# Other fills for the attention phase, another closing of its page pools and a staging ring of two slots, in a one-core hybrid trunk layer

## Chip, cores and metric

The kernel runs on one core of one Trainium2 chip. The metric is device time of an execution in microseconds (us), the median of several runs. A trace of one profiled execution shows what each engine did: PE is TensorE (matmuls), DVE is VectorE, ACT is ScalarE, POOL is GpSimd, SP is SyncE, which here issues most of the DMA transfers. Each engine works through its own list of instructions in order.

## What is computed

One layer over 2,064 tokens (16 meta tokens and 2,048 others) of 1,024 channels. One input projection feeds two branches; their results are joined, projected and added to the input.

```python
u = rmsnorm(h, norm_g) @ w_in
pool_in, pool_gate, c_q, c_kv, k_r, attn_gate = jnp.split(u, SPLIT_POINTS, axis=-1)
pool_out = silu(pool_gate) * pool_mixer(pool_in, pool_w, pool_scale)
# pool_mixer: 4 channel groups, mean over the last 2/4/8/16 tokens minus the token,
# then a 128x128 map per group
q  = rmsnorm(c_q,  q_norm_g)  @ w_q_b      # 4 heads, 128 plain + 64 rotary
kv = rmsnorm(c_kv, kv_norm_g) @ w_kv_b
attn = mla_attention(q_nope, q_rope, k_nope, k_rope, v, chunk_id)   # mask by chunks of 64
attn_out = silu(attn_gate) * attn
h = h + concatenate([pool_out, attn_out]) @ w_out
return rmsnorm(h, final_norm_g)[:, 16:]
```

## The kernel before

The kernel has three phases that overlap. First the columns of the input projection that attention needs (queries, keys and values compressed) are made for all tokens. Then attention goes over chunks of 64 tokens, late ones first, by groups of four chunks: the groups 5, 6, 7, 4, 3 and 2 in the order of the loop `for c in seq` (the first two groups have been done earlier). Last come the remaining 1,536 columns of the input projection ("the projection"), the pooling branch, the gates and the output projection, in blocks of 256 tokens.

One attention step is `scores(c, p)` for chunk c and head pair p: score matmuls on PE (names `s14_...`), maxima on DVE, exponentials on ACT into a page `p`, a split of it into two 16-bit halves (a page `hl`; ACT, POOL and DVE), and a transposing DMA, issued by SP, from `hl` to a page `pt`. `pv(c)` multiplies the pages by the values (`o14`), and once a group has four chunks `vproj` makes its attention result (`av`). `pv` is written a number of steps behind the scores of its chunk, the lag (0 or 1). The pages come in turn from rings that several pools make up: `set_pages` takes a list of pools with counts for (p, hl, pt), for example ATT1 = (2, 4, 2). Query preparation of a group (`qprep`, matmuls `qa`, `qp`, `qt`) is written ahead of the chunk named in QAT.

The projection works on twelve blocks of 128 columns, taken as six pairs: pairs 0 to 3 are a pooling group's channels with their gate, pairs 4 and 5 are two attention gates each. Text commands set their order, in the table PREP behind chosen chunks of attention and in the list TAIL behind attention:

- `a0` (`load_w`): the two weight blocks of pair 0 are loaded by SP into the staging ring (names `wr...`) and ACT takes their maxima; `b0` (`scale_w`): PE transposes the maxima (`wmx`), DVE works out a power of two, and ACT, DVE and POOL write the weights as two 16-bit halves (`w...`);
- `x0` (`load_x`): the 256 (272 for block 0) input columns of block 0 are loaded in two halves into the same staging ring (`yr0_0`, `yr0_4`), DVE multiplies them by the norm, ACT and POOL write two 16-bit halves (`xx`);
- `03`: block 0, pair 3 (`pair`): 24 matmuls of 128x256 for each of the two column blocks (`mp0_3` and `mp0_7`), then for a pooling group window sums on DVE (`pool_in`), a gate (`gate`), and one pair later the pooling map (`pool_out`, `pm0_3`); for attention gates, a product with the attention result;
- `o0` (`load_wo`): a slice of the output weights through the staging ring (`wor0`); ACT casts it, DVE subtracts, which gives two halves (`wo0`);
- `p0` and `q0` (`op_prep`, `op`): 128 tokens of the output projection, 48 matmuls of 128x512 (`op0_0`, `op0_1`); the residual rows go through the staging ring as well (`xr0`).

FILL says behind which chunk a pair of the list `fill` is written. A scheduler orders each engine's instructions by its own simulated times, so what is written behind a chunk may be interleaved with it. `raw` hands out staging slots: all loads go through it in turn, and one that comes round waits until the slot's last reader is done. The ring has two slots in pool c1 and, once pool mixp is open behind attention, a third.

Of the kernel before, what the change touches and what calls it, by code (L numbers as in the profile page):

```python
# [16 lines left out]
P = 128  # L17
# [21 lines left out]
B1_LAG = 1  # L39
B2_LAG = 0  # L40
ATT1 = (2, 4, 2)
ATT2 = (4, 4, 7)
ATT3 = (1, 1, 1)
NS = 6
QB = "m"
FILL = {13: 1, 12: 1, 11: 1, 9: 1}
XSC = 9
# [15 lines left out]
QAT = {22: 6, 26: 7, 30: 4, 19: 3, 15: 2}  # L63
CLOSE = 17
TAIL = """b3 a4 a5 03 b4 13 b5 04 o0 14 o1 05 o2 x2 15 o3 x3 20 o4 21 o5 o6 22 o7 g 23 p0 24 25 q0 x4
          p1 30 q1 p2 31 q2 32 p3 33 q3 34 35 p4 x5 40 q4 41 p5 42 q5 43 p6 44 q6 45 p7 x6 50 q7 51 p8 52 q8 53 p9 54 q9 55
          p10 x7 60 q10 61 p11 62 q11 63 64 65 70 71 72 p12 73 q12 p13 74 75 q13 p14 q14 p15 q15"""
PREP = {17: 'a0', 16: 'b0 x0', 15: 'a1', 14: 'b1 a2', 13: 'b2', 12: 'x1', 10: 'a3'}

# [20 lines left out]
def hymba(tc, hT, hcat, tab, w_tok, w_m, w_out, wqT, wqr, wkT, wv, pool_w,  # L90
# [453 lines left out]
    def raw(cols, name):  # L544
        n = cnt[0]
        cnt[0] += 1
        pool, b = (cpools[0], 2) if len(cpools) == 1 or n % 3 < 2 else (cpools[1], 1)
        return pool.tile([P, cols], F32, name=name, tag="wr", bufs=b, padded_shape=[P, 1088])

    def load_x(i):  # L550
        o, n = SUBS[i]
        if "x" not in cw:
            cw["x"] = kx.tile([P, 2, 4352], F16, name="xx", tag="khi", bufs=1, padded_shape=[P, 2, 4352])
        x = cw["x"][:, i % 2, :2 * KT * n].rearrange("p (a k t) -> p a k t", a=2, k=KT)
        xh, xl = x[:, 0], x[:, 1]
# [13 lines left out]
    def load_w(pi):  # L569
        for e in range(2):  # L570
            m = MORDER[2 * pi + e]
            if pi == 4:
                wr = f(cpools[1].tile([P, D], F32R, name=f"wr{m}", tag="mh", bufs=2))
            else:
                wr = raw(D, f"wr{m}")
            nc.sync.dma_start(out=wr, in_=w_m[m])
            for n in range(2):
                junk = cw["pool"].tile([P, 512], F16, name=f"wa{m}_{n}", tag="wa", bufs=1)
                nc.scalar.activation(out=junk, in_=wr[:, n * 512:n * 512 + 512], func=AF.Abs, accum_out=wmx[:, pi, e, n:n + 1])
            wts[m] = (wr, 2 * pi + e)  # L580

    def scale_w(pi):
# [7 lines left out]
        for e in range(2):  # L590
            m = MORDER[2 * pi + e]
            wr, at = wts[m]
            wp = cpools[0 if pi < 3 else 1].tile([P, 2, D], F16, name=f"w{m}")
            sc = wsc[:, at:at + 1]
# [21 lines left out]
    def pool_in(g, i, ps):  # L616
        n = SUBS[i][1]
        c1, carry = cw["pool"], cw["carry"]
        u = c1.tile([P, 16 + n], F32, name=f"u{i}_{g}", tag="u", bufs=2, padded_shape=[P, 288])
# [20 lines left out]
    def gate(m, i, ps):  # L640
        gt = cw["pool"].tile([P, G], F32, name=f"gt{i}_{m}", tag="gt", bufs=3)
        th = cw["pool"].tile([P, G], F32, name=f"th{i}_{m}", tag="th", bufs=2)
        nc.scalar.activation(out=th, in_=ps[:, :G], func=AF.Tanh, scale=whalf[:, wts[m][2]:wts[m][2] + 1])  # L643
# [15 lines left out]
    def pre_c(pool):  # L659
        cpools.append(pool)  # L660
        cw["pool"] = pool
        cw["carry"] = pool.tile([P, H, 16], F32, name="carry")
        nc.gpsimd.memset(cw["carry"], 0.0)

    def load_pw():
        pool = cw["pool"]
        pw_r = raw(H * P, "pw_r")
# [18 lines left out]
    def pair(i, pi):  # L686
        m0, m1 = MORDER[2 * pi], MORDER[2 * pi + 1]
        if i not in mixg:
            mixg[i] = cpools[i % 3 // 2].tile([P, H, G], F32, name=f"mix{i}", tag="mix", bufs=1 if i % 3 == 2 else 2)
        q0 = mproj(m0, i)  # L690
# [112 lines left out]
    c1 = None  # L803
    fill = [(0, 0), (0, 1), (0, 2), (1, 0), (1, 1), (1, 2)]
    for c in seq:
        if c in QAT:
            qprep(QAT[c])
        for p in range(2):
            step(c, p, B1_LAG if not c1 else B2_LAG)
        if c == CLOSE:  # L810
            flush()
            close_pool(att2_cm)
            set_pages((att1, ATT1), (att3, ATT3))
            c1_cm, c1 = open_pool("c1", side="right")
# [88 lines left out]
```

## Time and profile before

| | us |
|---|---|
| median of 3 runs (918.52 to 921.26) | 919.92 |
| profiled execution | 919.55 |
| its span in the profile | 917.8 |
| PE busy, whole span | 863.5 (94%) |
| DVE, ACT, POOL busy | 525.1, 454.2, 329.5 |

Three stretches of the span: up to 481 us attention goes on, from 481 to 570.5 us the projection runs without attention up to the first output matmul, and from there to 913 us projection and output projection alternate. The span lies 1.75 us below the profiled execution's own time. An idle time of an engine counts where it is on the way to the end; PE is that engine here, so its waits and the clock that it was granted are read first.

### The profile page before, as it was taken

Reading aid. Unit: us, or ns where it says so; the run is one execution under the profiler, and the core shown is the slowest. Engines: PE = TensorE matmul, PEld = TensorE weight load, DVE = VectorE, ACT = ScalarE, POOL = GpSimd, SP = SyncE. Lnnn points to the kernel's source line nnn. Section 1 sums busy time; section 2 is a strip of 40 time slices with the busy share of each in tenths; the row PEclk is TensorE's granted clock in tenths of the full one; section 3 lists DMA queues with packets and bytes.
Section 4 is the critical chain, followed back from the end, with each engine's and each line's share of the span. In section 5 each row is a group of like instructions: output and inputs, shape, how many; then the busy total and the mean of one; then the engine's idle time right before and its main releaser. Section 6 shows DMA issues by size and latency. Waiting matters only on the chain. (4 is left out here: it accounts for less than half of the span.)

```text
span 917.8 us, 16168 instructions
## 1 busy us (share of the span) xinstructions
PE 863.5 (94%) x5849; PEld 750.6 (82%) x5849; DVE 525.1 (57%) x1224; ACT 454.2 (49%) x1189; POOL 329.5 (36%) x520
## 2 busy tenths in 40 slices
PE   9899899899999999778898979999999999999996
PEld 8798778888888888666696868888888888888885
DVE  5566678857666665866854985255444443534332
ACT  6576657757767755857545763122322313223121
POOL 2576542625446442442421573221311413212020
PEclk9999999999999999979997989999999999999999
DMA  8765435967898687495572352211211211210011
GB/s 265 231 196 161 116 56 110 162 133 135 147 154 146 127 153 155 74 209 128 134 157 75 99 176 67 92 46 54 92 46 46 98 63 54 96 55 13 11 55 50
DMA packets 206955, 101.79 MB, mean 111 GB/s; under 512 B 169257, under 2 KB 196363, under 8 KB 206875
## 3 DMA queue, kind: packets, MB, share of 16 engines
q1 hardware_dynamic: 187392, 93.30, 42.8%
q10 hardware_dynamic: 19483, 7.47, 3.4%
q8 instruction: 46, 0.75, 0.4%
q14 instruction: 34, 0.28, 0.1%
HBM read 55.60 MB, written 8.43 MB: 70 GB/s over the span
## 5 line engine op out<-in xcount | busy, mean ns | idle before, releaser
L612 PE MATMUL mp<-xx,w 128*128 128x256 f16 (+1 forms) x2304 | 268.4, 276 | 11.5 <-ACT xx L565 6.3
L612 PEld LDWEIGHTS <-w 128*128 128x128 f16 x2304 | 224.6, 99 | 47.2 <-issue 12.6
L737 PE MATMUL op<-wo,mh 128*128 128x512 f32 (+1 forms) x528 | 159.3, 384 | 0.0
L464 POOL TENSOR_TENSOR hl<-p,hl 128x512 f16<-128x512 f32 (+4 forms) x104 | 102.6, 1008 | 116.4 <-ACT hl L462 115.0
L459 ACT ACTIVATE p<-s,st 128x512 f32<-128x512 f32 (+8 forms) x168 | 99.1, 599 | 68.4 <-DVE st L444 53.8
L737 PEld LDWEIGHTS op<-wo,mh 128*128 128x128 f32 x528 | 97.2, 188 | 18.6
L438 DVE TENSOR_REDUCE st<-s 128x1 f32<-128x512 f32 (+6 forms) x154 | 89.1, 590 | 17.7 <-PE s L436 16.7
L495 PE MATMUL o<-pt,vh 128*128 128x256 f16 x544 | 91.9, 273 | 2.2 <-DVE ol L498 1.2
L739 DVE TENSOR_TENSOR xr<-op,xr 128x512 f32<-128x512 f32 (+1 forms) x33 | 22.3, 676 | 117.8 <-PE op L737 117.8
L462 ACT CAST hl<-p 128x512 f16<-128x512 f32 (+6 forms) x168 | 82.2, 538 | 7.9 <-DMA pt<-hl 5.9
L495 PE MATMUL o<-pt,vl 128*128 128x256 f16 x272 | 74.1, 273 | 0.0
L741 ACT ACTIVATE osq<-xr 128x512 f16<-128x512 f32 (+1 forms) x33 | 20.3, 616 | 98.3 <-DVE xr L739 83.3
L495 PEld LDWEIGHTS <-vh 128*128 128x128 f16 x544 | 51.9, 98 | 12.1 <-issue 4.6
L643 ACT ACTIVATE th<-mp,whalf 128x256 f32<-128x256 f32 x64 | 30.1, 471 | 55.4 <-PE mp L612 52.6
L737 PE MATMUL op<-wo,ml 128*128 128x512 f32 x144 | 56.1, 390 | 0.0
L464 DVE TENSOR_TENSOR hl<-p,hl 128x512 f16<-128x512 f32 (+7 forms) x64 | 45.4, 710 | 12.7 <-ACT hl L462 12.2
L432 PE MATMUL s<-klo,qh 128*128 128x512 f32 (+9 forms) x116 | 45.0, 388 | 3.4 <-DVE gt L645 3.3
L566 POOL TENSOR_TENSOR xx<-yr,xx 128x512 f16<-128x512 f32 (+1 forms) x32 | 41.4, 1308 | 15.6 <-ACT xx L565 15.6
L562 DVE SCALAR_TENSOR_TENSOR yr<-yr,gxs,rbc 128x256 f32<-128x256 f32 (+1 forms) x64 | 34.9, 604 | 19.4 <-DMA yr<-hT_in 19.4
L737 PE MATMUL op<-wo,ml_odd 128*128 128x512 f32 (+1 forms) x120 | 45.0, 375 | 0.0
L434 PE MATMUL s<-klo,ql 128*128 128x512 f32 (+9 forms) x116 | 43.1, 371 | 0.0
L433 PE MATMUL s<-klo,qh 128*128 128x512 f32 (+9 forms) x116 | 42.7, 368 | 0.0
(213 smaller groups left out, 1807.4 us busy)
## 6 DMA issues: line engine op xcount, KB each, us to landing
xt<-hcat_in SPq DMA_DIRECT2D x16, 512.0 KB, 5.0
xr<-hcat_in SPq DMA_DIRECT2D x16, 512.0 KB, 3.7
raw<-hT_in SPq DMA_DIRECT2D x15, 512.0 KB, 4.8
out_dram<-xr SPq DMA_DIRECT2D x15, 512.0 KB, 2.6
yr<-hT_in SPq DMA_DIRECT2D x14, 512.0 KB, 3.8
wr<-w_m_in SPq DMA_DIRECT2D x12, 512.0 KB, 3.8
rb<-rd ACTq DMA_DIRECT2D x32, 128.0 KB, 4.4
wor<-w_out_in SPq DMA_DIRECT2D x8, 512.0 KB, 4.2
```

Source lines behind the costliest of these rows:

```text
L432: nc.tensor.matmul(ps[:, :w], lhsT=q(qh), rhs=kt[:, 0, 0, sl], start=True, stop=False)
L433: nc.tensor.matmul(ps[:, :w], lhsT=q(qh), rhs=kt[:, 1, 0, sl], start=False, stop=False)
L434: nc.tensor.matmul(ps[:, :w], lhsT=q(ql), rhs=kt[:, 0, 0, sl], start=False, stop=False)
L438: nc.vector.reduce_max(out=mx[:, bi:bi + 1], in_=ps[:, :w], axis=AX.X)
L459: nc.scalar.activation(out=pr[:, o:o + w], in_=pss[bi][:, :w], func=AF.Exp, bias=nb_, accum_out=sm[:, bi:bi + 1] if nb > 1 else tot)
L462: nc.scalar.copy(out=hl[:, 0, sl], in_=pr[:, sl])
L464: eng.tensor_tensor(out=hl[:, 1, sl], in0=pr[:, sl], in1=hl[:, 0, sl], op=ALU.subtract)
L495: nc.tensor.matmul(ps[:, :2 * P], lhsT=v, rhs=x, start=i == 0, stop=i == len(ops) - 1)
L562: nc.vector.scalar_tensor_tensor(out=xr[:, k - k0], in0=xr[:, k - k0], scalar=gxs[:, k:k + 1], in1=rbc, op0=ALU.mult, op1=ALU.mult)
L566: nc.gpsimd.tensor_tensor(out=xl[:, k:k + 2], in0=xr[:, k - k0:k - k0 + 2], in1=xh[:, k:k + 2], op=ALU.subtract)
L612: nc.tensor.matmul(ps[:, :n - sk], lhsT=a[:, k], rhs=x[:, k, sk:n], start=e == 0, stop=e == 3 * KT - 1)
L737: nc.tensor.matmul(ps[:, :w], lhsT=x[:, k], rhs=y[:, sl], start=i == 0, stop=i == 3 * KT - 1)
```

## The change

- The attention phase: lag 1 throughout; ATT2 and ATT3 are cut differently (their sum with ATT1 is 7, 9 and 10 pages, as before); behind chunk 28 pages come from ATT1 and ATT3 alone (4, 7, 7). Pool c1 opens behind chunk 19 (before: 17), with no flush ahead of it.
- The fills are pairs 4 and 5 of block 0 and pair 4 of block 1 (three pairs, before six); weights of pairs 4 and 5 are prepared in attention, those of pairs 0 to 3 behind it.
- The first input columns have a tile of their own in c1 (`x0`), reused later by the output projection's `mh`; later columns go to `xx` as before.
- The staging ring has two slots throughout. The last weights' second way through the `mh` slots is gone.
- The pooling branch's tiles (carry, windows, pooling weights, mix) move from c1 to mixp, which is there only behind attention.

```diff
-B2_LAG = 0
+B2_LAG = 1
-ATT2 = (4, 4, 7)
-ATT3 = (1, 1, 1)
+ATT2 = (3, 2, 3)
+ATT3 = (2, 3, 5)
-FILL = {13: 1, 12: 1, 11: 1, 9: 1}
+FILL = {15: 1, 13: 1, 11: 1}
-CLOSE = 17
-TAIL = """b3 a4 a5 03 b4 13 b5 04 o0 14 o1 05 o2 x2 15 o3 x3 20 o4 21 o5 o6 22 o7 g 23 p0 24 25 q0 x4
...
-PREP = {17: 'a0', 16: 'b0 x0', 15: 'a1', 14: 'b1 a2', 13: 'b2', 12: 'x1', 10: 'a3'}
+LASTLONG = 28
+CLOSE = 19
+TAIL = """b0 w a1 15 24 b1 25 a2 00 10 b2 20 a3 01 11 b3 21 o0 02 o1 12 o2 22 o3 03 o4 13 o5 x3 23 o6 p0 o7 g
...
+PREP = {18: 'a4', 17: 'b4 x0', 16: 'a5', 15: 'b5', 14: 'x1', 12: 'x2', 10: 'a0'}
...
-        pool, b = (cpools[0], 2) if len(cpools) == 1 or n % 3 < 2 else (cpools[1], 1)
-        return pool.tile([P, cols], F32, name=name, tag="wr", bufs=b, padded_shape=[P, 1088])
+        return cpools[0].tile([P, cols], F32, name=name, tag="wr", bufs=2, padded_shape=[P, 1088])
...
-        if "x" not in cw:
-            cw["x"] = kx.tile([P, 2, 4352], F16, name="xx", tag="khi", bufs=1, padded_shape=[P, 2, 4352])
-        x = cw["x"][:, i % 2, :2 * KT * n].rearrange("p (a k t) -> p a k t", a=2, k=KT)
+        if i == 0:
+            x = cw["pool"].tile([P, 2 * KT * n], F16, name="x0", tag="x0", bufs=1)
+        else:
+            if i == 1:
+                cw["x"] = kx.tile([P, 2, 4352], F16, name="xx", tag="khi", bufs=1)
+            x = cw["x"][:, i % 2, :2 * KT * n]
+        x = x.rearrange("p (a k t) -> p a k t", a=2, k=KT)
...
-            if pi == 4:
-                wr = f(cpools[1].tile([P, D], F32R, name=f"wr{m}", tag="mh", bufs=2))
-            else:
-                wr = raw(D, f"wr{m}")
+            wr = raw(D, f"wr{m}")
...
-            wp = cpools[0 if pi < 3 else 1].tile([P, 2, D], F16, name=f"w{m}")
+            wp = cpools[0 if pi >= 4 else 1].tile([P, 2, D], F16, name=f"w{m}")
...
-        c1, carry = cw["pool"], cw["carry"]
+        c1, carry = cpools[1], cw["carry"]
...
-    fill = [(0, 0), (0, 1), (0, 2), (1, 0), (1, 1), (1, 2)]
+    fill = [(0, 4), (0, 5), (1, 4)]
...
-            step(c, p, B1_LAG if not c1 else B2_LAG)
+            step(c, p, B1_LAG)
+        if c == LASTLONG:
+            set_pages((att1, ATT1), (att3, ATT3))
         if c == CLOSE:
-            flush()
             close_pool(att2_cm)
-            set_pages((att1, ATT1), (att3, ATT3))
             c1_cm, c1 = open_pool("c1", side="right")
             pre_c(c1)
```

How the order moves at three places (line numbers of the changed kernel are 1 to 3 higher). PE where the first input columns are first used: `mp0_0` and `mp0_8` are projection matmuls of block 0, `o15` the value product of chunk 15, `s12` and `s14` scores, `qp2` the query preparation of group 2. Before:

```order
L495 MATMUL o15_5138<-pt15_2_5087,vc_122 128x256
L612 LDWEIGHTS w0_4924
L612 MATMUL mp0_0_5423<-xx_4942,w0_4924 128x272
...
L612 LDWEIGHTS w4_4930
L612 MATMUL mp0_4_5460<-xx_4942,w4_4930 128x256
...
L432 MATMUL s12_0_0_5490<-klo_115,qh3_4218 128x384
```

Now:

```order
L347 MATMUL qp2_4954<-wrh_126,cl2_4916 128x256
L613 LDWEIGHTS w8_4738
L613 MATMUL mp0_8_5162<-x0_4750,w8_4738 128x256
...
L613 LDWEIGHTS w9_4744
L613 MATMUL mp0_9_5192<-x0_4750,w9_4744 128x256
...
L433 MATMUL s14_0_0_5225<-klo_115,qh3_4218 128x512
```

The first use stands ahead of the scores of chunk 14 where it stood ahead of those of chunk 12, and right behind the query preparation; it is of pair 4 instead of pair 0.

SP, the loads of the staging ring behind attention (weights `wr`, output weights `wor`, input columns `yr`, residual rows `xr`). Before:

```order
L576 DMA wr8_6419<-w_m_in 128x1024
L576 DMA wr9_6425<-w_m_in 128x1024
L576 DMA wr11_6437<-w_m_in 128x1024
L576 DMA wr10_6431<-w_m_in 128x1024
L679 DMA wor0_6711<-w_out_in 128x1024
L679 DMA wor1_6778<-w_out_in 128x1024
L560 DMA yr2_0_6851<-hT_in 128x4x256
L560 DMA yr2_4_6861<-hT_in 128x4x256
L679 DMA wor2_6845<-w_out_in 128x1024
L679 DMA wor3_6934<-w_out_in 128x1024
L560 DMA yr3_0_6940<-hT_in 128x4x256
L679 DMA wor4_7028<-w_out_in 128x1024
```

Now:

```order
L577 DMA wr3_6623<-w_m_in 128x1024
L577 DMA wr7_6629<-w_m_in 128x1024
L680 DMA wor0_6880<-w_out_in 128x1024
L680 DMA wor1_6960<-w_out_in 128x1024
L680 DMA wor2_7040<-w_out_in 128x1024
L680 DMA wor3_7120<-w_out_in 128x1024
L680 DMA wor4_7202<-w_out_in 128x1024
L680 DMA wor5_7284<-w_out_in 128x1024
L564 DMA yr3_0_7290<-hT_in 128x4x256
L564 DMA yr3_4_7300<-hT_in 128x4x256
L680 DMA wor6_7388<-w_out_in 128x1024
L723 DMA xr0_7398<-hcat_in 128x1024
```

Six output weights stand in a row and block 3's input columns behind them, the ring being two slots instead of three.

PE at the first output matmuls, halves `op0_0` and `op0_1` of the first 128 tokens. Before:

```order
L737 MATMUL op0_0_7412<-wo6_7110,ml0_7275 128x512
L737 MATMUL op0_0_7412<-wo7_7190,mh0_7274 128x512 x2
L737 MATMUL op0_0_7412<-wo7_7190,ml0_7275 128x512
L737 MATMUL op0_1_7440<-wo0_6710,mh0_7274 128x512 x2
L737 MATMUL op0_1_7440<-wo0_6710,ml0_7275 128x512
...
L737 MATMUL op0_1_7440<-wo7_7190,mh0_7274 128x512 x2
L737 MATMUL op0_1_7440<-wo7_7190,ml0_7275 128x512
...
L612 MATMUL mp3_0_7504<-xx_4942,w0_4924 128x256
```

Now:

```order
L738 MATMUL op0_0_7408<-wo5_7283,ml0_7393 128x512
L738 MATMUL op0_1_7436<-wo0_6879,ml0_7393 128x512
L738 MATMUL op0_1_7436<-wo1_6959,mh_7392 128x512 x2
L738 MATMUL op0_1_7436<-wo1_6959,ml0_7393 128x512
L738 MATMUL op0_0_7408<-wo6_7387,mh_7392 128x512
L738 MATMUL op0_1_7436<-wo2_7039,mh_7392 128x512 x2
L738 MATMUL op0_1_7436<-wo2_7039,ml0_7393 128x512
...
L738 MATMUL op0_1_7436<-wo6_7387,mh_7392 128x512 x2
L738 MATMUL op0_1_7436<-wo6_7387,ml0_7393 128x512
...
L613 MATMUL mp3_0_7469<-xx_5318,w0_6137 128x256
...
L738 MATMUL op0_0_7408<-wo7_7400,mh_7392 128x512
L738 MATMUL op0_1_7436<-wo7_7400,mh_7392 128x512
```

Before, the 48 output matmuls stood in a row behind all of block 2; now they go slice by slice, with projection matmuls of block 3 between those on output weights 6 and on output weights 7.

## Rows read from the trace of the kernel before

**Rows 1.** Busy time by stage: length, engines (instructions), granted clock, DMA share, GB/s.

```profile
360.00:481.00 121.00, 100.75 (x740) 87.62 (x738) 82.62 (x208) 74.45 (x205) 42.09 (x63) 0.94 0.66 144
481.00:570.50 89.50, 78.55 (x638) 67.09 (x637) 62.09 (x119) 48.96 (x99) 36.71 (x40) 0.90 0.36 110
570.50:913.00 342.50, 339.75 (x2295) 291.29 (x2293) 137.27 (x256) 89.35 (x211) 79.90 (x122) 1.00 0.17 57
```

Engines in these rows: PE, its weight loads, DVE, ACT, POOL.

**Rows 2.** The same view, PE alone, the stretches at half clock.

```profile
393.20:403.45 10.25, 6.01 (x20) 0.50 1.21 221
454.65:458.06 3.41, 3.29 (x16) 0.50 0.00 1
485.37:495.60 10.23, 8.67 (x36) 0.50 0.00 1
543.40:550.22 6.82, 4.26 (x19) 0.50 0.69 203
```

**Rows 3.** Waits of PE, 360 to 481 us: total, times, longest.

```profile
PE mp L612 <- ACT xx L565: 6.3, 1, 6.3
PE s L432 <- DVE gt L645: 3.3, 1, 3.3
PE qt L360 <- POOL qra L356: 2.9, 2, 2.2
PE qp L346 <- DVE ql L338: 1.4, 1, 1.4
PE pm L655 <- DVE at L520: 1.4, 1, 1.4
```

**Rows 4.** Timelines of PE, SP, ACT: start, length, instructions, [idle before].

```profile
373.79 1.05 PE L79 MATMUL wmx<-ident,wmx 128*128 128x128 f32 x8
...
389.05 0.33 SPq L668 DMA_DIRECT2D pw_r<-pool_w_in  x1
...
390.81 0.52 SPq L560 DMA_DIRECT2D yr<-hT_in  x1
...
396.75 1.19 ACT L565 CAST xx<-yr 128x544 f16<-128x544 f32 x2
...
486.74 2.00 PE L79 MATMUL wmx<-ident,wmx 128*128 128x128 f32 x8
...
495.35 0.33 SPq L576 DMA_DIRECT2D wr<-w_m_in  x1
```

**Rows 5.** Timeline of SP, 519 to 546 us: issues into the staging ring.

```profile
520.33 0.34 SPq L679 DMA_DIRECT2D wor<-w_out_in  x1
526.96 0.34 SPq L679 DMA_DIRECT2D wor<-w_out_in  x1
530.33 0.38 SPq L560 DMA_DIRECT2D yr<-hT_in  x1
533.83 0.33 SPq L679 DMA_DIRECT2D wor<-w_out_in  x1
540.70 0.33 SPq L679 DMA_DIRECT2D wor<-w_out_in  x1
542.90 2.65 SPq L679 DMA_DIRECT2D wor<-w_out_in  x2
```

**Rows 6.** Timeline of PE, 560 to 585 us.

```profile
565.39 5.41 PE L612 MATMUL mp<-xx,w 128*128 128x256 f16 x48
570.56 0.71 PE L737 MATMUL op<-wo,mh 128*128 128x512 f32 x2
...
581.57 3.67 PE L612 MATMUL mp<-xx,w 128*128 128x256 f16 x32
```

**Rows 7.** DMA issues (KB, us to landing) and a cast, 481 to 570.5 us.

```profile
wr<-w_m_in SPq DMA_DIRECT2D x12, 512.0 KB, 3.8
...
wor<-w_out_in SPq DMA_DIRECT2D x8, 512.0 KB, 4.2
...
L680 ACT CAST wo<-wor 128x1024 fp32r<-128x1024 f32 x8 | 8.3, 1040 | 5.9 <-DMA wor<-w_out_in 5.9
```

**Rows 8.** Waits of PE, 481 to 570.5 us.

```profile
PE pm L655 <- ACT plh L636: 5.3, 2, 4.7
```

More of the change, by code (lines that the diff above doesn't have):

```diff
@@ L63 @@
 QAT = {22: 6, 26: 7, 30: 4, 19: 3, 15: 2}
-CLOSE = 17
-TAIL = """b3 a4 a5 03 b4 13 b5 04 o0 14 o1 05 o2 x2 15 o3 x3 20 o4 21 o5 o6 22 o7 g 23 p0 24 25 q0 x4
-          p1 30 q1 p2 31 q2 32 p3 33 q3 34 35 p4 x5 40 q4 41 p5 42 q5 43 p6 44 q6 45 p7 x6 50 q7 51 p8 52 q8 53 p9 54 q9 55
-          p10 x7 60 q10 61 p11 62 q11 63 64 65 70 71 72 p12 73 q12 p13 74 75 q13 p14 q14 p15 q15"""
-PREP = {17: 'a0', 16: 'b0 x0', 15: 'a1', 14: 'b1 a2', 13: 'b2', 12: 'x1', 10: 'a3'}
+LASTLONG = 28
+CLOSE = 19
+TAIL = """b0 w a1 15 24 b1 25 a2 00 10 b2 20 a3 01 11 b3 21 o0 02 o1 12 o2 22 o3 03 o4 13 o5 x3 23 o6 p0 o7 g
+          q0 30 p1 q1 31 p2 32 q2 33 x4 p3 34 q3 35 p4 40 q4 41 x5 p5 42 q5 43 p6 44 q6 45 p7 50 q7 51 x6 p8 52 q8 53 p9 54 q9 55
+          p10 60 q10 61 x7 p11 62 q11 63 64 65 70 71 72 p12 73 q12 p13 74 75 q13 p14 q14 p15 q15"""
+PREP = {18: 'a4', 17: 'b4 x0', 16: 'a5', 15: 'b5', 14: 'x1', 12: 'x2', 10: 'a0'}
 def f(ap):
@@ L641, in gate @@
         gt = cw["pool"].tile([P, G], F32, name=f"gt{i}_{m}", tag="gt", bufs=3)
-        th = cw["pool"].tile([P, G], F32, name=f"th{i}_{m}", tag="th", bufs=2)
+        th = cw["pool"].tile([P, G], F32, name=f"th{i}_{m}", tag="tg", bufs=1)
         nc.scalar.activation(out=th, in_=ps[:, :G], func=AF.Tanh, scale=whalf[:, wts[m][2]:wts[m][2] + 1])
@@ L651, in pool_out @@
     def pool_out(g, i, plh, pll, gt):
+        if i not in mixg:
+            mixg[i] = cpools[1].tile([P, H, G], F32, name=f"mix{i}", tag="mix", bufs=3)
         pwh, pwl = cw["pw"]
@@ L661, in pre_c @@
         cw["pool"] = pool
-        cw["carry"] = pool.tile([P, H, 16], F32, name="carry")
-        nc.gpsimd.memset(cw["carry"], 0.0)
     def load_pw():
-        pool = cw["pool"]
+        pool = cpools[1]
         pw_r = raw(H * P, "pw_r")
@@ L687, in pair @@
         m0, m1 = MORDER[2 * pi], MORDER[2 * pi + 1]
-        if i not in mixg:
-            mixg[i] = cpools[i % 3 // 2].tile([P, H, G], F32, name=f"mix{i}", tag="mix", bufs=1 if i % 3 == 2 else 2)
         q0 = mproj(m0, i)
@@ L707, in op_prep @@
     def op_prep(t):
-        mh = cpools[1].tile([P, D], F32R, name=f"mh{t}", tag="mh", bufs=2).rearrange("p (k t) -> p k t", k=KT)
+        if t == 0:
+            cw["mh"] = cw["pool"].tile([P, 2, KT, P], F32R, name="mh", tag="x0", bufs=1, padded_shape=[P, 2, KT, 136])
+        mh = cw["mh"][:, t % 2]
         if t % 2 == 0 or t < 3:
@@ L817, in hymba @@
             {"a": load_w, "b": scale_w, "x": load_x}[u[0]](int(u[1]))
-            if u == "b0":
-                load_pw()
         for _ in range(FILL.get(c, 0)):
@@ L829, in hymba @@
     cpools.append(mxp)
+    cw["carry"] = mxp.tile([P, H, 16], F32, name="carry")
+    nc.gpsimd.memset(cw["carry"], 0.0)
     while fill:
@@ L837, in hymba @@
             {"p": op_prep, "q": op}[u[0]](int(u[1:]))
+        elif u == "w":
+            load_pw()
         elif u[0] in "abxo":
```

## Prediction

> **What bounds the kernel now.** I read the stretches by stage first, to see where TensorE (PE) is not the limit. From 570.50 to 913.00 us it works 339.75 of 342.50 us at a granted clock of 1.00, so a change finds nothing to win there. Ahead of it stand 360 to 481 us, the last attention chunks with the first projection work among them, with 100.75 busy of 121.00 us, and 481 to 570.50 us, the projection without attention up to the first output matmul, with 78.55 of 89.50 us [rows 1]. Idle there is 20.25 and 10.95 us. Then come the stretches at the lower of the two clocks (0.50, 1.2 GHz), each just behind an idle stretch: their busy times of 6.01, 3.29, 8.67 and 4.26 us would be half at full clock, so 3.0, 1.65, 4.3 and 2.1 us are lost [rows 2]. I call idle plus lost clock waste: 24.9 us in the first stretch, 17.4 in the second, 42.3 in all. That is the whole prize. No other engine is full in either: VectorE (DVE), the busiest, has 82.62 of 121.00 and 62.09 of 89.50 us [rows 1], so it delays by the order of its work, not by the sum.
>
> The waits of PE say whose waste it is [rows 3]: 6.3 us for the first normalised input columns (the first block's projection matmul waits for the cast of x), 3.3 for a gate on DVE that stands ahead of a score's work, 2.9 and 1.4 for the query preparation, 1.4 for an attention result; the other 4.95 us of the 20.25 are small ones.
>
> **The change part by part.** Matmul work is the same. The fills of the attention phase go from six pairs of channels to three, as matmuls that the order places before the last attention result 277 to 232. At 0.108 us each (48 from 565.39 to 570.56 us [rows 6]) that is 5 us, moved from the first stretch to the second; at equal cover it costs nothing. It does take pooling chains (window sums on DVE) out of a stretch where DVE is the busiest helper.
>
> First, the wait for x0. Today block 0's weights are measured for their scale on PE at 373.79 us, but their staging slots are free only when the pooling weights' load issues, 389.05 us; x0's first half is issued behind it and a page transpose at 390.81, DVE normalises it when it has landed, ScalarE casts it from 396.75 to 397.94 in two parts [rows 4], and PE waits 6.3 us for the first of them. Scale to release is therefore 15.3 us there, and about 8.6 us (486.74 to 495.35) for the weights whose scaling meets an emptier ACT and POOL [rows 4]. In the new order the pool with these buffers opens two chunks earlier and the chain starts two chunks earlier, but with it moves the first consumer: PE now wants x0 right after the query preparation of group 2, ahead of the scores of chunk 14, where it used to be ahead of those of chunk 12. So it is the distance that counts. On SyncE (SP) the load also stands behind all six page transposes of chunk 16, and whatever holds it in SP's queue holds the transposes of chunk 15 behind it. From PE's scale matmul to the use I count 13.5 to 15 us of scheduled matmuls. The chain needs 8.6 to 15.3 us to the release and 6.5 from the load's issue to the first part's cast (390.81 to 396.75, and half of 1.19) [rows 4]: 15.1 to 21.8 us. Against the 13.5 to 15 us the wait is between 0 and about 8 us; I take 4.0, the middle, as neither row's surroundings are those of the new place, and its lost clock by proportion 1.9 instead of 3.0. That gives 3.4 us.
>
> Second, the query wait of 2.9 us [rows 3] goes: 20 score matmuls and 24 gate matmuls now stand between the query's two products, about 8 us of work. The other, 1.4, stays.
>
> Third, the gate. The score that waits for a gate on DVE, 3.3 us, the half-clock matmuls behind it (1.65 [rows 2]), a small wait of 1.2 between them and the 1.4 for an attention result [rows 3] come from window sums and gates that are queued on DVE ahead of softmax steps. The late chunks (10 to 8) have no fill any more, so all four go: 7.5 us. What they cost without fill is not in the trace; PE then runs at the pace of softmax. I bound it by 0 (no waits of PE are listed from 300 to 360 us, where chunks run unfilled) and 6 (the gap that x0 leaves today), and take 3. For the new tile switch at the second x (its buffer is the keys' space, shared with what frees late) I put 2, between 0 and 4, the landing of one load [rows 7].
>
> First stretch: 24.9 − 3.4 − 2.9 − 7.5 + 3 + 2 = 16.1, a gain of 8.8 us.
>
> Fourth, the pages: after chunk 28 only 4, 7 and 7 (before 7, 9 and 10 until chunk 17, then 3, 5 and 3). For chunks 19 to 16 this is less, where PE has no listed wait today; bounds 0 and 6 (again the largest gap today), taken 1.5, since the ring still holds more than one full chunk.
>
> Fifth, the tail, which decides the rest. It begins with block 0's channels, and the staging ring has two slots instead of three (weights for the last pair had two more of their own). Every weight pair takes a turn: 3.8 us landing [rows 7], the maximum of its columns on ScalarE and 8.6 to 15.3 us to the release [rows 4], about 16.5 us in all. PE has 488 projection matmuls (53 us) and 8 pooling products and scale matmuls (5 us) between the last attention result and the first matmul on the last weights (mp0_3). The staging slot of these is free at 11 + 3 x 16.5 = 61 us, PE arrives at 58 plus early waits of 3.5 plus some clock, 64 us: some 3 us later. From there eight output weights, two halves of block 3's x and the first residual share two slots. In one of them stand output weights 0, 2, 4, a half of x, output weights 6 and 7. A turn of output weights is 4.2 us landing, 1.04 us cast [rows 7], a subtraction on DVE and the next issue. From issue to issue in one slot I read eight turns, the shortest 6.6 us (520.33 to 526.96), the longest 9.07 (533.83 to 542.90) [rows 5], their mean 7.4; I take 7.1, without the longest. A turn of x is 10.4 us (530.33 to 540.70) [rows 5]. Output weights 7 are ready at 3 x 7.1 + 10.4 + 7.1 + 5.3 = 44 us after the slot came free. PE has 174 projection matmuls (18.8 us), 44 output matmuls at 0.23 (48 from 570.56 to 581.57 us [rows 6]; 10.1) and 3 pooling products (1.1), 30 to 31 us to its first matmul on them. 44 − 3 − 31 = 10 us of wait. Early turns 3.5, lost clock 2, small ones 0.5: 16.0 instead of 17.4, a gain of 1.4. The 5.3 us that PE waits today for casts of pooled channels behind output weight work [rows 8] are not all won: the new order puts casts of output weights in front of such casts too.
>
> One page has another price for such a load. The Trainium skill, "DMA: Bandwidth & Descriptors", section "Anatomy of one DMA — SWDGE (gpsimd) path", has a fit for another path of about 2.0 us plus bytes over 436e3 per us, by estimate 3.2 us for these 512 KB. The rows say 3.8 and 4.2, for loads from SP. By the page's fit a turn would be 1 us shorter, and five of them would give back 5 us of the 10; the rows decide.
>
> Sixth, the steady state behind 570 us holds residual and output rows in two slots, not three. Nothing waits there now; bounds 0 and 3 (a turn of x instead of one of output weights, 10.4 for 7.1 [rows 5]), taken 0.5, since 11 us of output matmuls [rows 6] cover a landing of some 4.
>
> Sum, against the profiled execution's 919.55 us: −8.8 + 1.5 − 1.4 + 0.5 = −8.2, **911.4 us**; the median of the runs is 919.92, 0.4 above that execution, so I write 911.5.
>
> **The rivals.** *Slower, by the two-slot ring.* If each turn of output weights in the shared slot costs what a turn of x costs, 10.4 instead of 7.1 us, because its cast and subtraction queue behind gates and window sums that now stand in the tail, four turns add 13.2 us and the longer gaps some 2 us of clock: 926.7 us. It decides, that is the gain is gone, from a turn of 9.1 us on (8.2 over 4, above 7.1). For it: 9.07 us was read once already with three slots [rows 5]. Against it: the other seven turns and their mean. Chance 0.25. The Trainium skill says beside this ("Perfetto Trace Analysis", section "Optimization Strategy") that gaps which repeat on the engine that should be full can mean that SBUF holds too few buffers for the next tile. By it the tail would show several equal gaps, one a turn, and the time would be this rival's; the trace of before, with three slots, shows only one long wait there.
>
> *The same, the gap moves.* The wait for x0 is 8 us with 3 of clock (5.1 more than I took), and the unfilled chunks cost 6 (3 more): 919.6 us. For it: the consumer moved as far as the chain, and six transposes stand ahead. Chance 0.19.
>
> *A larger gain.* x0 is there (5.9 less) and the unfilled chunks cost nothing (3 less): 902.6. Chance 0.09.
>
> That the change doesn't do what it says I leave no chance of its own: the order shows the moves.
>
> **How the numbers follow.** Forecast 911.5 with 0.47, the three rivals with 0.25, 0.19 and 0.09. The forecast's own range is 904 to 916.5, x0 from 0 to 8 or a ring turn 1 us either way. The range from 900 to 927 takes in all three rivals' middles; what it leaves out, some 0.17, lies mostly above. A measurement of this kernel can tell about 0.3% (2.8 us) from no change. Faster by more: 0.47 + 0.09 = 0.56; within: 0.19; slower: 0.25.
>
> **What would show it.** PE's waits up to the last attention result should sum to some 14 us, with one wait of about 4 for x0 at the scores of chunk 14, none for a gate on DVE in the late chunks, and none from query transposes. In the tail some 10 us of waits for casts of output weights or what they hold up should stand around the first output matmuls, and turns in the ring of 7 us. I am wrong if the tail's waits exceed 18 us, if page waits show in chunks 19 to 16, or if PE waits for residuals behind the output's start.

## The result and the profile after

The changed kernel takes 907.1 us (median of four runs, 905.4 to 908.96), the kernel before 920.59 us beside it: a ratio of 0.9857, 95% interval 0.9827 to 0.9887. That is 13.5 us less where 8.4 were forecast; the profiled executions differ by 11.1 us (908.45 and 919.55). The two were compared once more later (0.987, 0.9842 to 0.9897; run `again`, below).

To see where it came from I cut both traces at the same instructions of PE. The lengths in us:

| stretch | before | after | difference | less 7.4 of moved work |
|---|---|---|---|---|
| start to the scores of chunk 19 | 311.90 | 312.75 | +0.9 | |
| to the value product of chunk 18 | 43.38 | 46.14 | +2.8 | |
| to the last attention result | 125.78 | 110.44 | −15.3 | −7.9 |
| to the first channels of block 6, pair 3 | 338.57 | 338.53 | 0.0 | −7.4 |
| to the end | 98.17 | 98.84 | +0.7 | |

The moved work is what PE now does behind attention and not in it: 45 projection matmuls at 0.109 us (4.9; the prediction counted these alone), 9 of the pooling map at 0.117 (1.1), 8 transposes of weight maxima at 0.111 (0.9), and 72 projection matmuls that are 272 columns wide where 256 now stand, 7 ns each (0.5): 7.4 us. So attention gave 7.9 us, its first chunks took back 2.8, and the tail gave 7.4.

Three runs below (`again`, `mh128`, `mhs32`) have the same order of instructions on every engine as the changed kernel. In their traces the attention stretch takes 109.45, 107.51 and 110.48 us beside 110.44 here, and PE's idle in the tail is 6.46, 6.10 and 4.65 us beside 7.65 here. A difference of up to 3 us between two single traces therefore shows nothing.

Busy time by stage in the changed kernel (length, then PE, its weight loads, DVE, ACT, POOL, granted clock, DMA share, GB/s), from the scores of chunk 15 to the last attention result, to the end of the first output step's last long wait, and on. They answer to [rows 1]:

```profile
361.99:469.33 107.34, 93.27 (x693) 81.96 (x692) 69.25 (x181) 66.79 (x187) 46.45 (x60) 0.95 0.74 149
469.33:571.24 101.91, 94.26 (x782) 80.94 (x780) 65.63 (x137) 52.94 (x110) 29.60 (x45) 1.00 0.31 94
571.24:902.00 330.76, 327.94 (x2212) 278.63 (x2211) 131.93 (x264) 90.29 (x209) 80.27 (x121) 1.00 0.19 62
```

Idle of PE is 14.1 us in the first of them (20.25 before) and 7.65 in the second (10.95 before), and in the second the granted clock is 1.00 throughout, where 0.90 stood before: the two half-clock stretches of the tail [rows 2] have no successor in this trace (in `mh128` and `mhs32` there is one, with 1.7 us lost). In attention there are two (PE alone, as in [rows 2]), one around the wait for a gate, one around the wait for pages, both listed below; half of their busy time, 4.6 us, is lost, as much as before:

```profile
415.85:422.68 6.83, 6.10 (x20) 0.50 0.44 117
460.23:463.64 3.41, 3.08 (x15) 0.50 0.36 70
```

PE's waits in attention, 300 to 480 us (total, times, longest), beside [rows 3]:

```profile
PE o L496 <- DMA pt<-hl: 4.1, 1, 4.1
PE s L433 <- ACT gt L648: 3.4, 1, 3.4
PE av L520 <- DVE qr L367: 2.9, 2, 1.7
PE mp L613 <- ACT x L569: 1.7, 1, 1.7
PE qa L335 <- DVE ol L499: 1.6, 1, 1.6
PE qt L361 <- POOL qra L357: 1.6, 1, 1.6
```

The wait for the first input columns fell from 6.3 to 1.7 us, with no half clock behind it; the two waits of group 2's query preparation are gone, and a new one of 1.6 (`qa`) stands in it. A gate still holds the scores, now at chunk 11, and the last value product waits for its transposed pages. In the tail, 480 to 580 us, beside [rows 8]:

```profile
PE op L738 <- ACT mh L718: 3.1, 1, 3.1
PE pm L658 <- ACT plh L637: 2.1, 1, 2.1
PE wmx L80 <- ACT wa L580: 1.5, 2, 1.1
PE pm L658 <- DVE pll L638: 1.0, 1, 1.0
```

No PE wait is listed behind 580 us. And yet the steady state is not the same: an output matmul of 512 columns starts 231.3 ns after the one ahead of it (mean of some 610 pairs behind 600 us) where it took 227.0 (some 630 pairs), while projection matmuls start every 109.35 ns in both. 792 output matmuls make 3.4 us of that, 2.5 of them ahead of block 6. Without it the tail would have given 9.9 us.

The staging slot that the prediction followed, issue by issue on SP, and the last output weights' cast on ACT:

```profile
528.21 0.33 SPq L680 DMA_DIRECT2D wor<-w_out_in  x1
534.84 0.33 SPq L680 DMA_DIRECT2D wor<-w_out_in  x1
540.87 0.33 SPq L680 DMA_DIRECT2D wor<-w_out_in  x1
546.78 0.38 SPq L564 DMA_DIRECT2D yr<-hT_in  x1
555.39 0.34 SPq L680 DMA_DIRECT2D wor<-w_out_in  x1
563.76 0.33 SPq L680 DMA_DIRECT2D wor<-w_out_in  x1
...
567.29 1.05 ACT L681 CAST wo<-wor 128x1024 fp32r<-128x1024 f32 x1 [4.64 <-DMA wor<-w_out_in]
```

Turns of 6.6, 6.0, 5.9, 8.6 (x) and 8.4 us, beside [rows 5]. The cast ends at 568.34 us, 40.1 after the slot came free; PE's first matmul on it starts at 569.30, without a wait, 1.0 us behind the cast's end.

### The profile page after: what moved, and what is told of

It reads as the page before. It is cut to its first block, busy times and chain, and to the rows that moved or that the text cites. A ratio compares the mean times of both kernels' runs of the same rounds, so it can differ in the third digit from the quotient of the medians.

```text
span 906.7 us, 16178 instructions
## 1 busy us (share of the span) xinstructions
PE 859.5 (95%) x5849; PEld 747.1 (82%) x5849; DVE 509.3 (56%) x1224; ACT 455.3 (50%) x1189; POOL 328.4 (36%) x520
## 5 line engine op out<-in xcount | busy, mean ns | idle before, releaser
L613 PEld LDWEIGHTS <-w 128*128 128x128 f16 x2304 | 222.0, 98 | 35.8 <-issue 7.2
L613 PE MATMUL mp<-xx,w 128*128 128x256 f16 x2016 | 233.0, 274 | 0.0
L738 PE MATMUL op<-wo,mh 128*128 128x512 f32 (+1 forms) x528 | 161.3, 388 | 3.1 <-ACT mh L718 3.1
L570 POOL TENSOR_TENSOR xx<-yr,xx 128x512 f16<-128x512 f32 x28 | 35.3, 1277 | 45.3 <-ACT xx L569 45.3
L465 DVE TENSOR_TENSOR hl<-p,hl 128x512 f16<-128x512 f32 (+7 forms) x64 | 43.5, 681 | 13.6 <-ACT hl L463 12.5
L433 PE MATMUL s<-klo,qh 128*128 128x512 f32 (+9 forms) x116 | 44.8, 386 | 4.5 <-ACT gt L648 3.4
L623 POOL COPY carry<-u 128x16 f32<-128x16 f32 x32 | 15.2, 475 | 85.2 <-ACT u L622 85.2
L566 DVE SCALAR_TENSOR_TENSOR yr<-yr,gxs,rbc 128x256 f32<-128x256 f32 (+1 forms) x64 | 32.9, 573 | 21.1 <-DMA yr<-hT_in 17.4
L702 POOL TENSOR_TENSOR at<-at,gt 128x256 f32<-128x256 f32 x32 | 23.5, 734 | 55.7 <-DVE gt L649 45.2
```

The costliest lines, as they stand in the source:

```text
L433: nc.tensor.matmul(ps[:, :w], lhsT=q(qh), rhs=kt[:, 0, 0, sl], start=True, stop=False)
L465: eng.tensor_tensor(out=hl[:, 1, sl], in0=pr[:, sl], in1=hl[:, 0, sl], op=ALU.subtract)
L566: nc.vector.scalar_tensor_tensor(out=xr[:, k - k0], in0=xr[:, k - k0], scalar=gxs[:, k:k + 1], in1=rbc, op0=ALU.mult, op1=ALU.mult)
L570: nc.gpsimd.tensor_tensor(out=xl[:, k:k + 2], in0=xr[:, k - k0:k - k0 + 2], in1=xh[:, k:k + 2], op=ALU.subtract)
L613: nc.tensor.matmul(ps[:, :n - sk], lhsT=a[:, k], rhs=x[:, k, sk:n], start=e == 0, stop=e == 3 * KT - 1)
L702: nc.gpsimd.tensor_tensor(out=t[:, m - 8], in0=t[:, m - 8], in1=gt, op=ALU.mult)
```

## The experiments

They ran on three chips: `mh128`, `ring3`, `tail2` and `long19` on one, `mhs32`, `b136`, `x1late` and `fill10` on the next, `again`, `close17`, `cf` and `f14m` on the last. Each is compared with the kernel before beside it (medians of 917 to 919 us), and stretches are read from its own trace. The changed kernel itself ran on the last of these chips alone (`again`).

**The output matmuls' 4 ns.** The left operand `mh` has a new place and new rows. First its rows:

```diff
-cw["mh"] = cw["pool"].tile([P, 2, KT, P], F32R, name="mh", tag="x0", bufs=1, padded_shape=[P, 2, KT, 136])
+cw["mh"] = cw["pool"].tile([P, 2 * KT * P], F32R, name="mh", tag="x0", bufs=1, padded_shape=[P, 2 * KT * 136]).rearrange("p (s k t) -> p s k t", s=2, k=KT)
```

> The changed kernel, with the two slots of the output projection's left operand mh packed in rows of 128 elements (512 bytes) instead of 136 (544 bytes). In the changed kernel an output matmul of 512 columns starts 231.5 ns after the one ahead of it, in the kernel before 226.7; nothing waits. Theory A (the wider rows of mh are slower to load as weights): the distance goes back to about 226.7 ns, 792 of them give 3.7 us, about 903.5 us. Rival B (something else in the place of the tiles or in the run itself): 231.5 ns and 907 us again.

905.14 us, ratio 0.9855 (0.9822 to 0.9888), and 233.4 ns: worse per matmul. Neither theory had that. It fits an effect of the address. By the addresses of the built programs, all rows of `mh` lay at 32 bytes past a multiple of 256 before; with packed rows they lie at 160 past it; with rows of 544 bytes each of the eight lies at another offset. So the next run moved the packed rows by 128 bytes:

```diff
-cw["mh"] = cw["pool"].tile([P, 2, KT, P], F32R, name="mh", tag="x0", bufs=1, padded_shape=[P, 2, KT, 136])
+cw["mh"] = cw["pool"].tile([P, 2 * KT * 136], F32R, name="mh", tag="x0", bufs=1)[:, 32:32 + 2 * KT * P].rearrange("p (s k t) -> p s k t", s=2, k=KT)
```

> The changed kernel with mh in rows of 512 bytes and begun 128 bytes further into its buffer: its rows then lie at 32 bytes past a multiple of 256 (as in the kernel before, and as the other operands), where rows of 512 bytes from the buffer's start lay at 160 past it and gave 233.3 ns from one output matmul to the next, the changed kernel's rows of 544 bytes 231.4, the kernel before 226.7. Theory A (the offset within 256 bytes decides): 226.7 ns, 576 and more matmuls some 4 ns shorter, 3.5 to 4 us less than the changed kernel. Rival B (the region of memory in which mh lies): 233 ns, no gain. Rival C (something of the program that is not mh): 231 to 233 ns.

227.1 ns, and 900.77 us, ratio 0.9807 (0.9776 to 0.9838). And the other way round, the wide rows in the kernel before, in its own place (the same buffers take a pair's weights `wr` ahead of it):

```diff
-wr = f(cpools[1].tile([P, D], F32R, name=f"wr{m}", tag="mh", bufs=2))
+wr = f(cpools[1].tile([P, D], F32R, name=f"wr{m}", tag="mh", bufs=2, padded_shape=[P, KT * 136]))
...
-mh = cpools[1].tile([P, D], F32R, name=f"mh{t}", tag="mh", bufs=2).rearrange("p (k t) -> p k t", k=KT)
+mh = cpools[1].tile([P, KT, P], F32R, name=f"mh{t}", tag="mh", bufs=2, padded_shape=[P, KT, 136])
```

> The kernel before, with its two mh buffers in rows of 544 bytes, as in the changed kernel, and otherwise the same: the cost of the rows' offset by itself. Theory A (offset within 256 bytes): each row lies at another offset, one of eight at 32, so the distance of output matmuls rises from 226.7 to 230 to 232 ns, 792 of them cost 3 to 4 us. Rival B (the region): 226.7 ns and the time of the kernel before.

231.4 ns; 920.46 us beside 917.15, ratio 1.0027 (1.0002 to 1.0052). Rows of the groups by line (count, busy us and mean ns of one), 600 to 850 us, for the changed kernel, then the packed rows, then those moved by 128 bytes, then the kernel before with wide rows; the length of one is modelled, its differences are those of the starts:

```profile
L738 PE MATMUL op<-wo,ml 128*128 128x512 f32 x83 | 32.7, 394 | 0.0
```

```profile
L738 PE MATMUL op<-wo,ml 128*128 128x512 f32 x82 | 32.5, 397 | 0.0
```

```profile
L738 PE MATMUL op<-wo,ml 128*128 128x512 f32 x81 | 31.5, 389 | 0.0
```

```profile
L737 PE MATMUL op<-wo,ml 128*128 128x512 f32 x80 | 31.6, 395 | 0.0
```

The place of `mh` decides: 128 bytes make the difference between 233.4 and 227.1 ns, and neither the region of memory nor the width of the rows as such does. Also matmuls on `ml`, which never moved off its offset, are longer: one operand's place slows the whole alternating row of matmuls. An offset has no fixed price of its own, though. Three matmuls on one row of `mh` (two on the row, one on `ml`) take 680 ns when every row lies at 32, 700 when every row lies at 160. With wide rows all eight rows are longer than 680 (685 to 711 ns in the changed kernel, 693 to 703 in `b136`, the first of them with the start of a half in it), the row at 32 too, and the row at 160 in the middle of `b136` takes 694. So more than a row's own offset plays in; what the rule is, and whether it counts from the right operand's place (32 past, too), was not told apart.

**The third staging slot.**

```diff
-return cpools[0].tile([P, cols], F32, name=name, tag="wr", bufs=2, padded_shape=[P, 1088])
+if len(cpools) == 1 or n % 3 < 2:
+    return cpools[0].tile([P, cols], F32, name=name, tag="wr", bufs=2, padded_shape=[P, 1088])
+return cpools[1].tile([P, cols], F32, name=name, tag="wr", bufs=1, padded_shape=[P, D])
...
-th = cw["pool"].tile([P, G], F32, name=f"th{i}_{m}", tag="tg", bufs=1)
+th = cw["pool"].tile([P, G], F32, name=f"th{i}_{m}", tag="rbc", bufs=1, padded_shape=[P, 272])
```

To make room, the gates' tanh (`th`) shares the buffer of the broadcast norms, and the order of the attention phase shifts a little with the edit.

> The changed kernel with a third staging slot once the attention is over (the gates' tanh shares the buffer of the broadcast norms to make room). Theory A (the two-slot ring sets the waits around the first output matmuls, as predicted): weight turns and output weights come sooner, the 7.7 us of idle between the last attention result and the end of the first output step fall to 3 or less, about 903 us. Rival B (the waits come from the order of work on DVE and ACT, not from the ring): idle stays at 6 to 9 us, 906 to 908 us.

908.43 us, ratio 0.9893 (0.9854 to 0.9932). The first output weights are issued 51.3 us behind the last attention result instead of 58.9, and PE's idle to the end of the first output step is 5.7 us:

```profile
469.16:566.31 97.15, 91.46 (x745) 77.31 (x743) 63.08 (x136) 51.49 (x107) 29.59 (x44) 1.00 0.32 99
```

That is 2 us less idle than in the profile above, but inside the 4.65 to 7.65 us of the four traces with the changed kernel's order. At equal work (less the moved work) the stretch from the last attention result to block 6 takes 330.7 us, and 331.1, 329.8 and 332.5 in the changed kernel, `again` and `mh128` (the last with the slowest output matmuls). So a third slot gives nothing here: rival B, though the idle lies just under its range and the time just above. One thing speaks for the chain of theory A. With the other waits around the first output matmuls nearly gone, PE's longest wait is now for a cast of output weights:

```profile
PE op L740 <- ACT wo L683: 2.0, 1, 2.0
```

**Three blocks between weight turns.**

```diff
-TAIL = """b0 w a1 15 24 b1 25 a2 00 10 b2 20 a3 01 11 b3 21 o0 02 o1 12 o2 22 o3 03 o4 13 o5 x3 23 o6 p0 o7 g
+TAIL = """b0 w a1 15 24 b1 25 a2 00 10 b2 a3 01 11 b3 20 o0 02 21 o1 12 o2 22 o3 03 o4 13 o5 x3 23 o6 p0 o7 g
...
```

> The changed kernel with block 2's first two pairs moved behind the last weights, so that two blocks instead of three stand between two weight turns. A weight turn is 15.7 us there, three blocks' matmuls are 15.6, two blocks' 10.4. Theory A (three blocks cover a turn, and that keeps PE busy and its clock up): waits of some 5 us before pairs 1, 2 and 3, stretches at half clock behind them, and no full return later: 912 to 918 us. Rival B (only the ring's total time up to the last output weights counts, the order in it does not): gaps ahead, but as much less idle around the first output matmuls: 905 to 909 us.

911.48 us, ratio 0.9921 (0.989 to 0.9951). From the last attention result to block 6 it takes 337.1 us at equal work, 4.6 to 7.3 more than the three traces above: most or all of what the tail had gained (338.6 before). PE's timeline and a stretch of the clock, where pair 1 waits for its weights' scaling:

```profile
486.30 0.49 PE L80 MATMUL wmx<-ident,wmx 128*128 128x128 f32 x2 [0.27 <-ACT wa L580]
489.74 0.41 PE L613 MATMUL mp<-x,w 128*128 128x272 f16 x1 [2.96 <-ACT w L597]
...
486.00:495.00 9.00, 5.40 (x25) 3.48 (x25) 4.22 (x12) 4.50 (x10) 2.27 (x2) 0.62 0.08 16
```

The time is just under theory A's range and clear of B's. What is lost at the weights is not given back at the output.

**The closing in two parts, undone.**

```diff
-LASTLONG = 28
-CLOSE = 19
+LASTLONG = 17
+CLOSE = 17
...
-PREP = {18: 'a4', 17: 'b4 x0', 16: 'a5', 15: 'b5', 14: 'x1', 12: 'x2', 10: 'a0'}
+PREP = {17: 'a4', 16: 'b4 x0', 15: 'a5', 14: 'b5', 13: 'x1', 11: 'x2', 10: 'a0'}
...
-FILL = {15: 1, 13: 1, 11: 1}
+FILL = {14: 1, 12: 1, 10: 1}
```

> The changed kernel with the first part of the page pools kept to chunk 17 and closed there, and the weights' and columns' loads and the fills one chunk later each (chunks 14, 12, 10 instead of 15, 13, 11): the closing in two parts undone, the rest as changed. Theory A (the earlier opening is what the attention gains by): 4 to 8 us slower than the changed kernel. Rival B (the gain lies in the gates as fills and in the tail, and the distance from chain to use counts, not the date): within 2 us of it, or faster by what the later third fill gives (1 to 3 us).

913.08 us, ratio 0.992 (0.9889 to 0.9952); the changed kernel beside it, 908.37:

> The changed kernel itself, beside the other runs on their chip. Expected 903 to 906 us, from the two runs with its order there (905.1 with 233.4 ns per output matmul, 903.5 with 231.3) and from 900.8 with 227.1 ns plus 3.4.

(The changed kernel is 2.4 us above what was expected; the runs that this was taken from stood on the two other chips.) 4.7 us slower, in theory A's range; the two intervals against the kernel before just touch (0.9842 to 0.9897 and 0.9889 to 0.9952). From the value product of chunk 18 to the last attention result it takes 117.05 us, the changed kernel beside it 109.45; 1.6 of the difference is more projection work. In PE's waits, 358.88 to 440 us, the query preparation of group 2 is back, and the turning of the softmax sums waits for DVE:

```profile
PE rt L380 <- DVE ri L378: 3.1, 1, 3.1
PE qp L347 <- DVE st L444: 2.2, 1, 2.2
PE qt L361 <- DVE ql L339: 2.1, 1, 2.1
```

`f14m`, below, has the first fill at the same chunk but the closing of the changed kernel, and lists none of the three. Still, the edit moves the closing, the short rings, the loads and all three fills together; what each of them costs was not told apart.

**The long rings kept longer.**

```diff
-LASTLONG = 28
+LASTLONG = 19
```

> The changed kernel with the long page rings (7, 9, 10) kept up to chunk 19 instead of chunk 28, so that the pool for the projection waits for the last long pages. From 324 to 349 us the changed kernel lost 2.8 us against before. Theory A (the short rings cost that): the loss in that stretch goes, but the projection's weights start later and x0 waits longer: between 904 and 909 us, the page part 2 to 3 us less. Rival B (lag and order, not the rings): the stretch loses 2.8 us as before, and the total is 907 or more.

909.2 us, ratio 0.9903 (0.9865 to 0.9941), while `mh128`, the changed order with slower output matmuls, took 905.14 on that chip. In the changed kernel the first chunks' 2.8 us are two waits: 1.6 for a query transpose (`qt`, at 335 us) and 1.2 before an attention result (at 348). With the long rings both are gone, but another stands at 358 us, inside the same stretch, before scores that wait for exponentials:

```profile
PE s L433 <- ACT p L460: 2.7, 1, 2.7
```

So PE idles 2.7 us there all the same. `close17`, whose rings are long to chunk 17, idles 1.9, of which 1.1 at that query transpose, and its stretch is 2.0 us longer than before. No run lists a wait for pages there. The 2.8 us are not shown to be a price of the shorter rings, nor are they cleared of it: the waits move with the order, and their cause stays open.

**The first use of x0.** Together with the faster place of `mh`:

```diff
-FILL = {15: 1, 13: 1, 11: 1}
+FILL = {14: 1, 13: 1, 11: 1}
```

> mh as in the faster layout, and the first fill behind chunk 14 instead of 15, so that the scores of chunk 14 stand ahead of the first use of x0 and not behind it. Theory A (the distance from the weights' chain to the first use sets the wait for x0, as the prediction had it): the wait for x0, 1.6 to 1.7 us in three of the runs with the changed order, is gone, and 1 to 3 us with it: 898 to 900. Rival B (the work is only in another order and the late chunks' waits stay or grow): 900 to 902.

905.14 us, ratio 0.9836 (0.9808 to 0.9863), where that place of `mh` alone has 0.9807 on another chip. PE's first matmul on x0 does not wait now, as the distance says; what waits for x0 is left with its later parts:

```profile
PE mp L613 <- POOL x L570: 1.0, 2, 0.7
PE mp L613 <- ACT x L569: 0.2, 1, 0.2
```

The fill's place is not the only thing that sets this wait: `mhs32`, with the fill at chunk 15, waits 0.2 us at the first use, as the matmuls ahead of it ran at half clock for 3.4 us and PE came later. Others stand in its place (2.9 before an attention result, 3.7 for exponentials), and attention is no shorter: rival B for the time, even above its range.

**The third fill and block 1's columns.** `fill10` sets the third fill behind chunk 10 instead of 11, `x1late` writes the loads of blocks 1 and 2 one chunk later, and `cf` is `fill10` with the faster `mh`.

```diff
-FILL = {15: 1, 13: 1, 11: 1}
+FILL = {15: 1, 13: 1, 10: 1}
```

> The changed kernel with the third fill (block 1, pair 4) behind chunk 10 instead of 11. PE's last wait in attention, 4.1 us for the transposed pages of chunk 8, and 4 us at a lower clock behind it, has only three projection matmuls ahead of it in the changed kernel. Theory A (the last chunks lack work in front of the page transposes): that wait goes to under 1 us, up to 6 us less at the last attention result, if chunks 11 and 10 without fill lose less than 2. Rival B (softmax paces all unfilled chunks alike): as much wait appears at the scores of chunks 11 and 10, no gain.

902.14 us, ratio 0.9829 (0.9792 to 0.9867). Where the changed kernel has a single wait of 4.1 us for pages, this trace has two of at most 1.6, with no lower clock behind them:

```profile
PE o L496 <- DMA pt<-hl: 3.1, 2, 1.6
```

That is no effect of the fill that can be told: `again` and `mh128`, with the changed kernel's own order, have 2.3 and 2.2 us in two waits there, the longest 2.0 and 1.9. Theory A wanted less than 1. With the faster `mh` the time is 901.64 us, 0.9815 (0.9787 to 0.9843), against 0.9807 without the moved fill, so a gain can't be told from none.

> Both that helped: mh at 32 past a multiple of 256 bytes (900.8 us alone) and the third fill behind chunk 10 (902.1 alone, against some 904 for the changed kernel). If the two add up: 898 to 899.5 us. If the wait for the last pages only moves into the tail: 900 to 901.

```diff
-PREP = {18: 'a4', 17: 'b4 x0', 16: 'a5', 15: 'b5', 14: 'x1', 12: 'x2', 10: 'a0'}
+PREP = {18: 'a4', 17: 'b4 x0', 16: 'a5', 15: 'b5', 13: 'x1', 11: 'x2', 10: 'a0'}
```

> The changed kernel with the loads of block 1's and 2's input columns written one chunk later each (behind chunks 13 and 11 instead of 14 and 12). In the changed kernel DVE stands from 411.6 to 414.3 us before the second half of block 1's columns, which land late, ahead of the softmax maxima of chunk 12, and PE waits 3.4 us at the scores of chunk 11 for a gate behind them, with 5 us at half clock after it. Theory A (that load in DVE's order is the cause): the wait at chunk 11 falls under 1 us and its half clock goes, 4 to 6 us less up to the last attention result. Rival B (the staging slots free no later, so the columns are only late at their first use): the wait moves to block 1's first matmul, no gain.

903.49 us, ratio 0.9845 (0.9803 to 0.9888), and the wait at chunk 11 stands unchanged:

```profile
411.21 0.45 PE L433 MATMUL s<-klo,qh 128*128 128x400 f32 x1 [3.40 <-ACT gt L648]
```

It tells nothing: in DVE's order the columns stand at the same place as before the edit, since the scheduler, not the line, decides. I had also misread the cause. DVE stands before the first half of the columns for 1.3 us; the second half it does not wait for but works on, and two of its eight multiplications take 1.4 us instead of 0.48, while POOL subtracts the first half. DVE and POOL of the changed kernel:

```profile
409.99 1.28 DVE L566 SCALAR_TENSOR_TENSOR yr<-yr,gxs,rbc 128x256 f32<-128x256 f32 x3 [1.31 <-DMA yr<-hT_in]
...
411.19 0.48 DVE L566 SCALAR_TENSOR_TENSOR yr<-yr,gxs,rbc 128x256 f32<-128x256 f32 x1
...
411.64 1.41 DVE L566 SCALAR_TENSOR_TENSOR yr<-yr,gxs,rbc 128x256 f32<-128x256 f32 x1
...
412.98 1.37 DVE L566 SCALAR_TENSOR_TENSOR yr<-yr,gxs,rbc 128x256 f32<-128x256 f32 x1
...
411.60 2.46 POOL L570 TENSOR_TENSOR xx<-yr,xx 128x512 f16<-128x512 f32 x2 [4.97 <-ACT xx L569]
```

That these delays, some 3.1 us in sum, make the wait of 3.4 us at chunk 11 is argued from the order (the maxima and the gate's product stand behind), not shown.

## Why the prediction was right, and where it was off

**Direction and range** held. In attention PE's idle came out at 14.1 us where 16.1 of waste less 1.9 of clock, 14.2, were forecast, and the stretch gave 7.9 us (8.9 in the trace of `again`) instead of 8.8. That the idle agrees to 0.1 us is luck, since the terms in it missed in both directions; and the clock gave nothing, 4.6 us lost instead of 1.9.

- *x0*: right in kind: the first use waits for the load, 1.7 us here, and not at all or 0.2 where the fill stands a chunk later or PE comes late (`f14m`, `mhs32`). The size, 4.0 with 1.9 of clock, was the middle of 0 to 8; it came out at 1.7 and none.
- *Queries*: the priced wait of 2.9 is gone, and so is the 1.4 that was to stay; a new one of 1.6 stands in the same preparation. With the closing, rings and fills of `close17` waits of this preparation come back.
- *The gate*: half wrong. The pooling chains left, but a gate on ACT and DVE still holds a score for 3.4 us, with 3.0 lost to the clock around it (half of 6.10). The prediction had none left.
- *Late chunks without fill*: taken at 3, found at 4.1 in one wait for pages with 1.5 of clock, and at 2.3 in `again`.
- *The second x*, taken at 2: no wait of PE for it is listed in attention. It is there only as DVE's work ahead of the gate.
- *Pages*: 1.5 was taken, 2.8 found in the first chunks, with no wait for pages listed; `long19` and `close17` leave the cause open.

**The tail** is the step that failed: a gain of 1.4 us was worked out, 7.4 measured, 9.9 without the slower output matmuls. Its mechanism, a chain of turns through one slot, is there and was nearly right in time: the slot came free 58.9 us after the last attention result (61 forecast), PE came to the last projection weights at 62.4 (64), and the last output weights were ready 40.1 us after the slot (44). What was mis-sized is the wait that comes of it, 44 − 3 − 31 = 10. With the measured times the same sum is 40.1 − 3.5 − 31.4, that is 5.2. And even this is not seen, because waits are not added when they run side by side: on its way PE had stood 6.2 us around the first output matmuls, for pooled channels and for `mh` behind work on DVE and ACT, and so came 1.0 us after the chain's end. That PE would have stood 5.2 us before the chain without these other waits is worked out, not shown; the third slot made chain and waits shorter together and gave no time. The early turns cost 1.5 us instead of 3.5, and the clock nothing instead of 2 (1.7 in two of the four traces with this order), because three blocks' matmuls just cover a weight turn of 15.7 us. `tail2` takes that cover away, and most or all of the gain is gone. The prediction counted these matmuls only as a sum against the turns, not turn by turn, and so missed what the change does best.

**The rivals.** The slower one priced a turn of output weights at 10.4 us; it was 5.9 to 8.4, and the ring did not decide. The sentence of the Trainium skill on repeating gaps ("Perfetto Trace Analysis", "Optimization Strategy") has nothing to act on here: the changed kernel's tail shows a few single waits and no row of equal gaps, one a turn. The rival without gain needed x0 to wait 8 us. The larger gain was nearly right about x0, wrong about the unfilled chunks, and did not have the tail.

**What nobody had listed** cost 3.4 us: the place of `mh`. The prediction put the steady state's risk on its ring (0.5 us); no wait is there at all. Put back to 32 bytes past a multiple of 256, the kernel takes 900.77 us, 0.9807 of the kernel before (0.9776 to 0.9838), beside 0.9857 and 0.987 for the changed kernel.

## What to carry to other kernels

Where loads come in turns, compare the matmuls between two turns with one turn, one by one: a cover that is just long enough kept the engine and its clock up here, and a total over all turns did not show it. Where two waits can run side by side, take the longer and do not add them. When a change moves an operand, compare the distance of matmuls in a stretch without waits; a few ns each are in no list of waits. Look in the new order for what an edit moved before trusting a run that it was meant to change, and take a second trace of the same order before reading a difference of 2 or 3 us between two traces.

## What the hardware showed

The left operand's place changed the pace of the f32 output matmuls with full clock and no wait: 227.0 and 227.1 ns with all its rows at 32 bytes past a multiple of 256 (two kernels), 233.4 with all at 160 past, 231.3 and 231.4 with eight different offsets (two kernels). The Trainium skill, "SBUF — State Buffer", section "Operand start alignment", lets an operand start at any multiple of its element size and says that this is about legality, not speed; all these layouts obey it, and the runs show a price of up to 2.8%.
